# Moving the rotary and residual sums of a hybrid decoder block into transfers that add at their destination

## Chip, cores and metric

One core of a Trainium2 chip. The metric is the device time of one execution in microseconds (us); with one core its span is that time. The kernel is written for the engines PE (matmul), DVE (vector), ACT (scalar), POOL and SP (which only issues transfers).

## What is computed

One layer of a decoder block on 2048 tokens of width 1024, all in float32, and a final norm. Cut from the reference:

```
u = rms_norm(h, norm1_gain)
x_lru, g_lru, q, k, v, g_ret = split(u @ w_in)
y_lru = rms_norm(rg_lru(conv(x_lru)) * gelu(g_lru))
qh, kh = rotary(q), rotary(k)          # concat(x1*cos - x2*sin, x2*cos + x1*sin)
y_ret = head_group_norm(retention(qh, kh, v)) * silu(g_ret)
h = h + concat(y_lru, y_ret) @ w_out
a, v = split(conv(rms_norm(h) @ ffn_up_w))
h = h + (gelu(a) * v) @ ffn_down_w
return rms_norm(h, final_norm_gain)
```

The sums that the change is about are the one inside `rotary` and the two with `h + ...`.

## The kernel before

The tokens are two groups g = 0, 1 of 1024 columns; everything is kept transposed, as tiles of 128 features by 1024 tokens (512 KB). A float32 matmul is made of three products of high and low parts: ACT rounds a tile to its high part (`wh`, `bh`), DVE subtracts it to get the low one (`wl`, and `raw` or `bl` for the activations). This is `split`. The big products run in units of a 2 x 2 block scheme with seven products instead of eight (`Unit`, L589; `PlainUnit` with eight, L725). One product is 12 matmuls of 128 x 512. A `Unit` uses the PSUM banks x (one), y and e (two each), and its helper `out` empties them: `u2`, `c11`, `c22`, `c21`, `c12` each take one quadrant out of `py`, `px`, `py`/`pe`, `py` and `pe`.

The stages are A (input projection with the recurrence and the retention heads), B (output projection), U (up-projection), D (down-projection, in three chunks c of its inner dimension, each a pass over both groups). They run as A for both groups, B for both, U for both, then D for c = 0, 1, 2. In the traced run A ends near 582 us, B runs to about 770, U to about 1700, D to about 2150, and the rest is the end.

Two classes empty the banks. `PlainOut` (L853) copies them to an `o` tile on ACT and adds the `pe` part on DVE. `AddOut` (L920), used by B and D, first loads the tile to be added to into a slot `res` (from the input x in B, from DRAM tile `h` in D) and lets DVE add every quadrant from PSUM into it. In D with c = 0 or 1 the result is stored as the next version of `h` in DRAM; with c = 2 and in B it goes to the norm, whose `add` squares it on ACT (`sqt`, `sqacc`) and sums on DVE. In B the result is also stored as the first version of `h`.

`rotate` (L1211) in a retention head swaps the two halves of a q or k tile by two transfers on SP into `sw`, multiplies both by the sine and cosine rows and adds, three operations on DVE.

The order on every engine is not that of the source: a planner at build time (`Flow`, L198) takes tasks with due times, models each engine's clock with the costs `cost_pe`, `cost_v`, `cost_a`, `cost_p` (L131 to L163), a lag of 0.2 us between engines, a transfer rate `RATE` and `SLOTS` buffers, and writes the order down. A longer or shorter modelled cost therefore moves instructions on all engines. Operations all carry line L127 in the profile (the helper that records them), and transfers L365. On each engine instructions run in the order given, so one that waits holds up those behind it; each transfer queue has eight semaphores in turn.

Of the kernel before, what the change touches and what calls it, by code (L numbers as in the profile page):

```python
# [39 lines left out]
EPS = 1e-6  # L40
SLOTS = 55
BANKS = {"x": 1, "y": 2, "e": 2, "sm": 3}
# [63 lines left out]
class Engine:  # L106
# [24 lines left out]
    def cost_pe(self, op, n, args, kw):  # L131
        if op == "transpose":
            return 0.13
        one = max(0.03, 0.0133 + n / 2400)
        if args[1].shape[0] == 64:
            one /= 2
        return one if args[1].dtype == F32R else 4 * one

    def cost_v(self, op, n, args, kw):
        if op == "tensor_tensor_scan":  # L140
            return 0.2 + 2.1e-3 * n
        if op in ("tensor_scalar", "tensor_copy", "memset"):
            return 0.15 + 0.535e-3 * n
        if op == "reciprocal":
            return 0.15 + 6.1e-3 * n
        if op == "bn_stats":
            return 0.3
        if op == "scalar_tensor_tensor":
            return 0.2 + 1.06e-3 * n
        return 0.15 + 1.05e-3 * n  # L150

    def cost_a(self, op, n, args, kw):
        us = 0.17 + 0.86e-3 * n
        if isinstance(kw.get("scale"), bass.AP):
            us += 0.1
        if isinstance(kw.get("bias"), bass.AP):
            us += 0.09
        if "accum_out" in kw:
            us += 0.2
# [38 lines left out]
class Flow:  # L198
# [33 lines left out]
    def ready(self, op):  # L232
        t = 0.0
        for name in op.reads:
            w = self.wrote.get(name)
            if w:
                t = max(t, w[0] + (0.0 if w[1] == op.eng else 0.2))
        for name in op.writes:
            for table in (self.wrote, self.read):
                w = table.get(name)  # L240
                if w:
                    t = max(t, w[0] + (0.0 if w[1] == op.eng else 0.2))
        return t

    def issue(self, op, start):
        us = op.us
        if op.eng == "a" and op.func is not None and op.func not in ANY_TABLE and op.func not in self.table:
            self.table = next(t for t in TABLES if op.func in t)
            us += 1.28
# [4 lines left out]
        if op.eng == "pe":  # L254
            end += 0.1
# [72 lines left out]
def hymba_block_kernel(ctx: ExitStack, tc: tile.TileContext, xh, xn, win, wout, wup, down, gates, vecs,  # L328
# [30 lines left out]
    def dma(dst, src, queue="sp"):  # L359
        n = 1  # L360
        for d in dst.shape:
            n *= d
        start = (nc.scalar if queue == "a" else nc.sync).dma_start
        writes = [] if dst.tensor.name == yT.tensor.name else parts(dst)
        return Op(queue, lambda: start(dst, src), ISSUE, writes, parts(src), kb=n / 256)  # L365

    class Dram:
# [118 lines left out]
    z_d = [[Dram(f"z{g}_{i}") for i in range(2)] for g in range(NG)]  # L486
    h_d = [[[Dram(f"h{g}_{c}_{i}") for i in range(KT // 2)] for c in range(4)] for g in range(NG)]
    u_d = [Blocks(f"u{g}") for g in range(NG)]
# [430 lines left out]

    class AddOut:  # L920


        def __init__(self, src, done):
            self.src, self.done = src, done
            self.t = {}
            self.there = [Event(), Event()]

        def load(self, t0):
            def fn(i):
                yield Until(t0 - 8)  # L930
                self.t[i] = yield Slot("res")
                yield from self.src[i][0].get(self.t[i], self.src[i][1])
                self.there[i].on = True

            for i in range(2):
                fl.spawn(fn(i), t0 - 4 + i)

        def add(self, i, n, src):
            yield self.there[i]
            t = self.t[i][:, half(n)]  # L940
            yield v.tensor_tensor(out=t, in0=t, in1=src, op=ALU.add)

        def quadrant(self, m, n, ps):
            yield from self.add(m, n, ps)
            free(ps)
            self.quads[m, n] = True
            if (m, 0) in self.quads and (m, 1) in self.quads:
                yield from self.done(m, self.t[m])

        def piece(self, m, c0, c1, ps):  # L950
            yield self.there[m]
            t = self.t[m][:, c0:c1]
            yield v.tensor_tensor(out=t, in0=t, in1=ps[:, 0:c1 - c0], op=ALU.add)
            free(ps)
            yield from self.pieces(m, self.t[m], c0, c1)
# [10 lines left out]
        def c22(self):  # L966
            u = self.unit
            yield from self.add(1, 1, u.y)
            u.done["c22a"].on = True
            yield u.t0 + 5 - SOON  # L970
            yield from self.add(1, 1, u.e)
            u.done["c22b"].on = True

        def c21(self):
            yield from self.add(1, 0, self.unit.y)
            free(self.unit.y)
            yield self.unit.done["c22b"]
            yield from self.done(1, self.t[1])

        def c12(self):  # L980
            yield from self.add(0, 1, self.unit.e)
            free(self.unit.e)
            yield self.unit.done["c11"]
            yield from self.done(0, self.t[0])

# [215 lines left out]
    class Head:  # L1201
# [354 lines left out]
    def stage_b(g):  # L1556
        st = RawStage("B", g, m_d[g])
        ng = NormGroup(V_N2, u_d[g].put, h_d[g][0], LATE * g)
        us = []
        for m in (range(KT // 2) if g == 0 else reversed(range(KT // 2))):  # L1560
            ms = (m, m + KT // 2)
            src = [(x_d[g][k // 2], k % 2) for k in ms]
            us.append(PlainUnit(st, (wout[ms[0]], wout[ms[1]]), AddOut(src, lambda i, t, ms=ms: ng.add(ms[i], t))))
        return st, us
# [6 lines left out]
    def stage_d(g, c):  # L1571
# [8 lines left out]

        ng = FinalGroup(V_NF, None) if final else NormGroup(V_NF, store, h_d[g][3])

        def partial(m, t):
            yield from h_d[g][c + 1][m // 2].put(m % 2, t)
            free(t)

        us = []
        for m in (range(KT // 2) if g == c % 2 else (KT // 2 - 1, *range(KT // 2 - 1))):
            ms = (m, m + KT // 2)
            src = [(h_d[g][c][k // 2], k % 2) for k in ms]  # L1590
            done = (lambda i, t, ms=ms: ng.add(ms[i], t)) if c == 2 else (lambda i, t, ms=ms: partial(ms[i], t))
            out = AddOut(src, done)
            out.pieces = lambda i, t, c0, c1, ms=ms: ng.piece(ms[i], t, c0, c1)
# [59 lines left out]
def _layout(inputs):  # L1653
# [32 lines left out]
    cos, sin = np.cos(ang).T, np.sin(ang).T  # L1686
    rope = np.stack([np.concatenate([cos, cos]), np.concatenate([-sin, sin])]).astype(f32)
    rope = rope.reshape(2, P, S // HT, HT).transpose(2, 0, 1, 3)
# [31 lines left out]
```

## Time and profile before

| what | us |
|---|---|
| median of 3 runs (2165.2 to 2167.5) | 2167.2 |
| the profiled execution, its span | 2165.3 |
| PE busy | 2143.6 |
| DVE busy | 1729.8 |
| ACT busy | 1226.1 |
| POOL busy | 38.3 |

The granted clock of PE is 0.999 of full speed. The profiled execution is read as follows: rows of one instruction have the start, the duration, engine, line, operation and its destination and sources, and in brackets how long the engine stood idle before it and whom it waited for. Rows of a group have a count, then busy time, the mean ns of one, and the idle time before. A wait is named by what PE wrote and read, so `PE px <- DVE raw` is a matmul into `px` that waited for DVE's `raw`.

### The profile page before, as it was taken

To read this page: it belongs to the slowest core of one execution; us is meant where nothing else is said; L and a number is where in the kernel's file an instruction comes from. 1 tells how busy PE (TensorE), PEld (TensorE's weight loads), DVE (VectorE), ACT (ScalarE), POOL (GpSimd) and SP (SyncE) were. 2 spreads that over 40 slices of the span, in tenths; PEclk is the share of its full clock that TensorE was granted. 3 is DMA by queue.
4 is the path that set the end of the run, shared out by engine and by line. 5 is a ranking of instruction groups with operands and counts; after the bars stand their busy time and mean duration, and the time that the engine had idled before them with its cause. 6 is when DMAs were issued, how large, how long until landed. Compare 5 with 4: busy or idle time off the path is not lost.

```text
span 2165.3 us, 26460 instructions
## 1 busy us (share of the span) xinstructions
PE 2143.6 (99%) x9848; PEld 1768.5 (82%) x9848; DVE 1729.8 (80%) x2185; ACT 1226.1 (57%) x1768; POOL 38.3 (2%) x32
## 2 busy tenths in 40 slices
PE   9999999999999999999999999999999999999998
PEld 7878887888878888888888888888888888888887
DVE  6999896877854789988878988787878977777776
ACT  6774668555652266666666866666666544334432
POOL 0000000000000000000000000000000000000000
PEclk9999999999999999999999999999999999999999
DMA  8966444431657935544233432322335777667674
GB/s 327 377 210 226 141 163 118 160 111 58 226 185 275 390 132 180 185 141 156 98 106 128 175 127 98 122 98 100 105 107 185 260 299 261 232 255 278 237 258 189
DMA packets 140768, 404.69 MB, mean 187 GB/s; under 512 B 15920, under 2 KB 20448, under 8 KB 140640
## 3 DMA queue, kind: packets, MB, share of 16 engines
q1 hardware_dynamic: 139344, 401.96, 52.7%
q8 instruction: 77, 1.26, 0.2%
q10 hardware_dynamic: 1296, 1.05, 0.1%
q14 instruction: 51, 0.42, 0.1%
HBM read 269.49 MB, written 125.07 MB: 182 GB/s over the span
## 4 chain that ended last, share of the span: by engine, by line
PE 92%; DVE 3%; DMA 3%; issue 1%; ACT 0%; SPq 0%; POOL 0%; DVEq 0%; ACTq 0%
PE py L127 33%; PE px L127 22%; PE pe L127 21%; PE pq L127 12%; PE po L127 1%; DMA raw<-in_dram 1%; PE pa L127 1%; PE pk L127 1%; PE sc L127 1%; PE pt L127 1%; DVE o L127 0%; PE mst L127 0%; DMA xt<-in_dram 0%; DMA x<-in_dram 0%; DVE wl L127 0%
## 5 line engine op out<-in xcount | busy, mean ns | idle before, releaser
L127 DVE TENSOR_TENSOR wl<-s,wh 128x1024 fp32r<-128x1024 f32 x172 | 210.2, 1222 | 113.4 <-ACT wh L127 108.7
L127 PE MATMUL px<-bh,wh 128*128 128x512 f32 x728 | 285.4, 392 | 1.4 <-DVE res L127 1.4
L127 PE MATMUL py<-bh,wh 128*128 128x512 f32 x728 | 285.9, 393 | 0.0
L127 PE MATMUL px<-raw,wh 128*128 128x512 f32 x728 | 283.8, 390 | 1.8 <-DVE raw L127 1.8
L127 PE MATMUL py<-bh,wl 128*128 128x512 f32 x728 | 283.9, 390 | 1.3 <-DVE wl L127 1.3
L127 PE MATMUL pe<-bh,wh 128*128 128x512 f32 x728 | 285.1, 392 | 0.0
L127 PE MATMUL pe<-raw,wh 128*128 128x512 f32 x728 | 283.7, 390 | 0.9 <-DVE raw L127 0.9
L127 PE MATMUL pe<-bh,wl 128*128 128x512 f32 x728 | 283.8, 390 | 0.7 <-DVE wl L127 0.7
L127 PE MATMUL py<-raw,wh 128*128 128x512 f32 x728 | 283.7, 390 | 0.0
L127 PE MATMUL px<-bh,wl 128*128 128x512 f32 x728 | 283.6, 390 | 0.0
L127 DVE SCALAR_TENSOR_TENSOR c<-o,vec,c 128x1022 f32<-128x1022 f32 x192 | 244.0, 1280 | 8.1 <-ACT c L127 3.3
L127 ACT CAST wh<-s 128x1024 fp32r<-128x1024 f32 x172 | 180.4, 1049 | 122.1 <-DVE s L127 107.1
L127 PE MATMUL py<-bh,wv 128*128 128x512 f32 x728 | 240.5, 391 | 1.9 <-DVE res L127 1.0
L127 ACT COPY o<-py 128x512 f32<-128x512 f32 x204 | 119.7, 587 | 167.1 <-PE py L127 163.5
L127 ACT CAST bh<-raw 128x1024 fp32r<-128x1024 f32 x158 | 162.2, 1050 | 68.0 <-DMA h<-res 27.4
L127 DVE TENSOR_TENSOR raw<-raw,bh 128x1024 fp32r<-128x1024 f32 x158 | 188.7, 1219 | 9.2 <-ACT bh L127 9.1
L127 PE MATMUL pq<-bh,wh 128*128 128x512 f32 (+1 forms) x432 | 168.0, 389 | 0.5 <-ACT bh L127 0.4
L127 PE MATMUL pq<-bh,wl 128*128 128x512 f32 (+1 forms) x432 | 165.2, 382 | 0.5 <-DVE wl L127 0.5
L127 PEld LDWEIGHTS py<-bh,wh 128*128 128x128 f32 x728 | 136.7, 188 | 33.1 <-issue 3.0
L127 PEld LDWEIGHTS py<-bh,wv 128*128 128x128 f32 x728 | 136.7, 188 | 32.7 <-ACT o L127 1.5
L127 PEld LDWEIGHTS px<-bh,wh 128*128 128x128 f32 x728 | 136.7, 188 | 31.3 <-DVE res L127 1.8
L127 PEld LDWEIGHTS py<-bh,wl 128*128 128x128 f32 x728 | 136.7, 188 | 30.8 <-DVE wl L127 2.1
(143 smaller groups left out, 3775.0 us busy)
## 6 DMA issues: line engine op xcount, KB each, us to landing
wa<-in_dram SPq DMA_DIRECT2D x86, 512.0 KB, 4.4
wb<-in_dram SPq DMA_DIRECT2D x86, 512.0 KB, 5.3
h<-res SPq DMA_DIRECT2D x56, 512.0 KB, 3.7
g_T<-t SPq DMA_DIRECT2D x96, 256.0 KB, 2.5
raw<-g_T SPq DMA_DIRECT2D x48, 512.0 KB, 5.7
res<-h SPq DMA_DIRECT2D x48, 512.0 KB, 7.2
g<-c SPq DMA_DIRECT2D x76, 256.0 KB, 4.2
raw<-g SPq DMA_DIRECT2D x38, 512.0 KB, 6.7
```

Of the source, the lines that this page charges most:

```text
L127: return Op(self.name, lambda: fn(*args, **kw), us, writes, reads, func=func)
```

## The change

Rotary: DVE multiplies the tile by the sine row into `sw` and by the cosine row in place, and two transfers issued by Pool add the halves of `sw`, swapped, into the tile (the sign of the sine row is set for that). Residual sums: `AddOut` becomes a `PlainOut`, so ACT copies the quadrants and DVE adds the `pe` part; a finished tile is then added by one transfer from Pool. In B and in D with c = 2 the transfer adds x or `h` from DRAM into the tile; in D with c = 0, 1 it adds the tile to `h` in DRAM, which is then one version only. The pieces of the `LastUnit` keep the old way. The planner's costs and lags are set to other numbers and there are 54 slots. The core of the diff:

```diff
-SLOTS = 55
+SLOTS = 54
...
+LAG = {"pe": 0.21, "v": 0.13, "a": 0.15, "p": 0.13, "dma": 0.08}
...
-        return 0.15 + 1.05e-3 * n
+        us = 0.068 + n / (1920 if op in ("tensor_scalar", "tensor_copy", "memset") else 960)
+        if any(isinstance(kw.get(k), bass.AP) for k in ("scalar", "scalar1")):
+            us += 0.06
+        return us
...
-        us = 0.17 + 0.86e-3 * n
...
+        us = 0.11 + (0.735e-3 if args[1].space == bass.MemoryType.PSUM else 0.82e-3) * n + 0.095 * aps
...
     def cost_p(self, op, n, args, kw):
-        return 0.1 if op == "dma_start" else max(1.0, 0.3 + 2.2e-3 * n)
+        return 0.8 + 0.105 * n if n < 16 else 0.15 + 2.25e-3 * n
...
-                t = max(t, w[0] + (0.0 if w[1] == op.eng else 0.2))
+                t = max(t, w[0] + (0.0 if w[1] == op.eng else LAG[w[1]]))
...
+    def add_to(dst, src):
...
+        return Op("p", lambda: nc.gpsimd.dma_start(dst, src, accum_op=ALU.add), 1.2, parts(dst), parts(dst) + parts(src),
+                  kb=n / 256)
...
-    class AddOut:
+    class AddOut(PlainOut):
...
-        def quadrant(self, m, n, ps):
-            yield from self.add(m, n, ps)
...
-        def u2(self):
-            yield from self.add(0, 1, self.unit.y)
-            self.unit.done["u2"].on = True
-
-        def c11(self):
-            yield from self.add(0, 0, self.unit.x)
-            free(self.unit.x)
-            self.unit.done["c11"].on = True
...
+        def first(self):
+            return self.whole(0, self.t1)
+
+        def second(self):
+            return self.whole(1, self.t2)
+
+        def whole(self, i, t):
+            d, j = self.src[i]
+            yield d.there[j]
+            if self.done is None:
+                yield add_to(d.t[:, j], t)
+                free(t)
+            else:
+                yield add_to(t, d.t[:, j])
+                yield from self.done(self.ms[i], t)
...
         def rotate(self, name, x):
-            sw = yield Slot("sw")
-            yield dma(sw[0:64], x[64:128]) + dma(sw[64:128], x[0:64])
...
+            sw = yield Slot("sw")
+            yield v.tensor_tensor(out=sw, in0=x, in1=sn, op=ALU.mult)
             yield v.tensor_tensor(out=x, in0=x, in1=cs, op=ALU.mult)
-            yield v.tensor_tensor(out=sw, in0=sw, in1=sn, op=ALU.mult)
-            yield v.tensor_tensor(out=x, in0=x, in1=sw, op=ALU.add)
+            yield add_to(x[0:64], sw[64:128]) + add_to(x[64:128], sw[0:64])
             free(sw)
...
-    nc = _bacc.Bacc("TRN2", target_bir_lowering=False, num_devices=1, dynamic_dma_scratch_size=256)
+    nc = _bacc.Bacc("TRN2", target_bir_lowering=False, num_devices=1, dynamic_dma_scratch_size=2048)
```

In the order of the engines PE keeps its matmuls. DVE gives up the 16 sums of the rotary and the 92 additions from `py` and `px` in D and those from `pq` in B; SP gives up the swaps and the loads of `res`. The 94 adding transfers (32 of half a tile, 62 of a tile) stand on Pool. On PE two places at the ends move: the broadcast `pb` at the start stands behind 120 matmuls, and at the end the first pair of `mst` stands behind the last twelve 256-wide matmuls instead of ahead of them.

The first place is SP at the end of stage B for group 1. A `w` is a weight tile of the last unit, `h1` are the stores of group 1's finished rows, `u0` the stores of group 0's normed rows, `in_0` the input x, `in_3` the weights. Before:

```order
L365 DMA u0_T4_1_136<-t34_6075 128x512
L365 DMA u0_22_1_138<-h_5910 128x512
L365 DMA h1_0_1_110<-res_5762 128x1024
L365 DMA res_5927<-in_0_dram 128x1024
L365 DMA h1_0_3_112<-res_5764 128x1024
L365 DMA w_6007<-in_3_dram 128x1024
L365 DMA res_6094<-in_0_dram 128x1024
L365 DMA w_6095<-in_3_dram 128x1024
```

The same place on SP in the changed kernel:

```order
L361 DMA u0_T4_1_120<-t34_6035 128x512
L361 DMA u0_22_1_122<-h_5887 128x512
L361 DMA h1_1_98<-o0_5920 128x1024
L361 DMA h1_3_100<-o1_6009 128x1024
L361 DMA w_5963<-in_3_dram 128x1024
L361 DMA w_6054<-in_3_dram 128x1024
L361 DMA raw_5964<-u0_11_0_109 128x1024
```

Both stores of `h1` now precede both loads of `w`, with no load of `res` between them, and the stores' tiles `o0_5920` and `o1_6009` are the ones that the adding transfers on Pool complete.

The second place is ACT in the last chunk of D, where a unit ends and the next one begins (the `sqt` and `sqacc` are the squares for the final norms, the copy `py<-px` is the start of a unit's y bank). Before:

```order
L127 ACTIVATE sqt_16021<-res_15673 128x1024
L127 CAST wh_16041<-wa_16035 128x1024
L127 COPY py_16071<-px_16056 128x512
L127 CAST wh_16091<-s1_16054 128x1024
L127 ACTIVATE sqt_16127<-res_15833 128x1024
L127 CAST wh_16142<-s1_16054 128x1024
L127 CAST wv_16147<-wb_16037 128x512
L127 ACTIVATE sqt_16150<-res_15832 128x1024
```

The same stretch of ACT in the changed kernel:

```order
L128 ACTIVATE sqacc_15932<-o1_15845 128x1024
L128 COPY o0_15946<-py_15863 128x512
L128 ACTIVATE sqt_15984<-o0_15810 128x1024
L128 COPY o0_15946<-px_15847 128x512
L128 CAST wh_15968<-wa_15963 128x1024
L128 COPY o1_15983<-py_15863 128x512
L128 COPY py_16003<-px_15988 128x512
L128 CAST wh_16009<-s1_15969 128x1024
L128 COPY o1_15983<-py_15863 128x512
```

The square of `o0_15810`, which the adding transfer completes, now stands between the copies of the next unit's quadrants `o0_15946` from `py` and from `px`; the latter frees the only x bank. Two more such places follow, for `o0_15946` and `o0_16216`.

More of the change, by code (lines that the diff above doesn't have):

```diff
@@ L132, in cost_pe @@
         if op == "transpose":
[L133 to L137, printed above, removed]
+            return 0.11
+        if args[1].dtype == F32R:
+            return 0.0133 + n / 2400
+        one = max(0.111, 0.0266 + n / 1200)
+        return one * (1.23 if args[1].shape[0] == 64 else 2)
     def cost_v(self, op, n, args, kw):
         if op == "tensor_tensor_scan":
-            return 0.2 + 2.1e-3 * n
-        if op in ("tensor_scalar", "tensor_copy", "memset"):
-            return 0.15 + 0.535e-3 * n
+            return 0.3 + 2.04e-3 * n
         if op == "reciprocal":
             return 0.15 + 6.1e-3 * n
[L146 to L149, printed above, removed]
-        return 0.15 + 1.05e-3 * n
+        us = 0.068 + n / (1920 if op in ("tensor_scalar", "tensor_copy", "memset") else 960)
+        if any(isinstance(kw.get(k), bass.AP) for k in ("scalar", "scalar1")):
+            us += 0.06
+        return us
     def cost_a(self, op, n, args, kw):
-        us = 0.17 + 0.86e-3 * n
-        if isinstance(kw.get("scale"), bass.AP):
+        aps = sum(isinstance(kw.get(k), bass.AP) for k in ("scale", "bias"))
+        us = 0.11 + (0.735e-3 if args[1].space == bass.MemoryType.PSUM else 0.82e-3) * n + 0.095 * aps
+        func = next((x for x in args if isinstance(x, AF)), None)
+        if aps and func is not None and func not in ANY_TABLE:
             us += 0.1
-        if isinstance(kw.get("bias"), bass.AP):
-            us += 0.09
         if "accum_out" in kw:
-            us += 0.2
+            us += 0.1
         return us
     def cost_p(self, op, n, args, kw):
-        return 0.1 if op == "dma_start" else max(1.0, 0.3 + 2.2e-3 * n)
+        return 0.8 + 0.105 * n if n < 16 else 0.15 + 2.25e-3 * n
 class Event:
@@ L241, in ready @@
                 if w:
-                    t = max(t, w[0] + (0.0 if w[1] == op.eng else 0.2))
+                    t = max(t, w[0] + (0.0 if w[1] == op.eng else LAG[w[1]]))
         return t
@@ L486, in hymba_block_kernel @@
     z_d = [[Dram(f"z{g}_{i}") for i in range(2)] for g in range(NG)]
-    h_d = [[[Dram(f"h{g}_{c}_{i}") for i in range(KT // 2)] for c in range(4)] for g in range(NG)]
+    h_d = [[Dram(f"h{g}_{i}") for i in range(KT // 2)] for g in range(NG)]
+    e_d = [[Dram(f"e{g}_{i}") for i in range(KT // 2)] for g in range(NG)]
     u_d = [Blocks(f"u{g}") for g in range(NG)]
@@ L930, in fn @@
                 yield Until(t0 - 8)
-                self.t[i] = yield Slot("res")
-                yield from self.src[i][0].get(self.t[i], self.src[i][1])
+                self.res[i] = yield Slot("res")
+                yield from self.src[i][0].get(self.res[i], self.src[i][1])
                 self.there[i].on = True
[L935 to L941, printed above, removed]
@@ L943, in quadrant @@
-        def quadrant(self, m, n, ps):
-            yield from self.add(m, n, ps)
[L945 to L948, printed above, removed]
+            if type(self.unit) is LastUnit:
+                for i in range(2):
+                    fl.spawn(fn(i), t0 - 4 + i)
         def piece(self, m, c0, c1, ps):
             yield self.there[m]
-            t = self.t[m][:, c0:c1]
+            t = self.res[m][:, c0:c1]
@@ L974, in c21 @@
[L974 to L984, printed above, removed]
+            yield from self.pieces(m, self.res[m], c0, c1)
+        def first(self):
+            return self.whole(0, self.t1)
@@ L1562, in stage_b @@
             src = [(x_d[g][k // 2], k % 2) for k in ms]
[L1563 removed]
+            us.append(PlainUnit(st, (wout[ms[0]], wout[ms[1]]), AddOut(g, ms, src, ng.add)))
         return st, us
@@ L1579, in store @@
                 free(pair[j])
[L1581 to L1585, printed above, removed]
+        ng = FinalGroup(V_NF, None) if final else NormGroup(V_NF, store, e_d[g])
         us = []
@@ L1589, in stage_d @@
             ms = (m, m + KT // 2)
-            src = [(h_d[g][c][k // 2], k % 2) for k in ms]
-            done = (lambda i, t, ms=ms: ng.add(ms[i], t)) if c == 2 else (lambda i, t, ms=ms: partial(ms[i], t))
-            out = AddOut(src, done)
+            src = [(h_d[g][k // 2], k % 2) for k in ms]
+            out = AddOut(g, ms, src, ng.add if c == 2 else None)
             out.pieces = lambda i, t, c0, c1, ms=ms: ng.piece(ms[i], t, c0, c1)
```

25 lines of the change are left out of this document (9 added, 16 removed).

## The prediction

> **What bounds the kernel now.** I read the first two rows of the page, then the waits of PE, then the busy time in 25-us stretches, and last single rows at the places the change touches. First the page: engines with busy time and share.
>
> ```profile
> span 2165.3 us, 26460 instructions
> PE 2143.6 (99%) x9848; PEld 1768.5 (82%) x9848; DVE 1729.8 (80%) x2185; ACT 1226.1 (57%) x1768; POOL 38.3 (2%) x32
> ```
>
> PE is busy in 2143.6 of 2165.3 us, and the change leaves its matmuls the same, so at most 21.7 us can be had. Of those the waits of PE hold a part (what it wrote and read, whom it waited for; us in total, times, longest); shown are the eleven largest of fourteen.
>
> ```profile
> PE px L127 <- DVE raw L127: 1.8, 1, 1.8
> PE y L127 <- DVE z L127: 1.5, 1, 1.5
> PE pb L127 <- POOL ms L127: 1.4, 2, 1.1
> PE px L127 <- DVE res L127: 1.4, 1, 1.4
> PE py L127 <- DVE wl L127: 1.3, 2, 1.0
> PE mst L127 <- DVE sqacc L127: 1.2, 1, 1.2
> PE py L127 <- DVE res L127: 1.0, 1, 1.0
> PE pt L127 <- DVE o L127: 0.9, 1, 0.9
> PE pe L127 <- DVE raw L127: 0.9, 1, 0.9
> PE py L127 <- ACT o L127: 0.8, 2, 0.4
> PE pe L127 <- DVE wl L127: 0.7, 1, 0.7
> ```
>
> These are 12.9 us, and 8.0 of them name DVE inside the stages (all but `z` at the start, `pb` and `mst` of the norms, and ACT's `o`). Where DVE is late is seen in the stretches (length, then busy PE, PEld, DVE, ACT, POOL with counts, PE clock, DMA share, GB/s).
>
> ```profile
> 150.00:175.00 25.00, 23.24 (x101) 18.38 (x100) 22.23 (x26) 8.72 (x13) 0.00 (x0) 1.00 0.97 301
> 725.00:750.00 25.00, 25.00 (x112) 20.72 (x111) 10.78 (x13) 6.34 (x7) 0.00 (x0) 1.00 1.01 385
> 1700.00:1725.00 25.00, 24.14 (x107) 19.58 (x105) 24.68 (x30) 8.19 (x10) 0.00 (x0) 1.00 0.50 170
> 2100.00:2125.00 25.00, 23.98 (x106) 19.57 (x105) 22.97 (x25) 7.16 (x8) 0.00 (x0) 1.00 0.93 344
> 1700.00:2150.00 450.00, 446.75 (x2017) 370.96 (x2016) 336.17 (x400) 170.94 (x189) 2.75 (x2) 1.00 0.68 248
> ```
>
> The clock is 1.00 throughout. In the down-projection (1700 to 2150) PE loses 3.25 us, with DVE packed where it loses them and ACT busy 171 of 450 us. In the out-projection around 725 PE loses nothing, but the DMA engines are full (share 1.01).
>
> **The change part by part.** The profiled execution spans 2165.3 us and the median of the runs is 2167.2, so I take the sum as a difference and apply it to the median. What a measurement of this kernel can tell from no change is about 0.2%, 4.3 us.
>
> *Residual sums of the down-projection.* DVE loses these additions from PSUM, and ACT gains copies of the kind in the third row.
>
> ```profile
> L127 DVE TENSOR_TENSOR res<-res,py 128x512 f32<-128x512 f32 x69 | 47.3, 685 | 32.0 <-PE py L127 31.6
> L127 DVE TENSOR_TENSOR res<-res,px 128x512 f32<-128x512 f32 x23 | 15.8, 685 | 18.9 <-PE px L127 18.9
> L127 ACT COPY o<-py 128x512 f32<-128x512 f32 x204 | 119.7, 587 | 167.1 <-PE py L127 163.5
> 1739.68 0.50 PE L127 MATMUL px<-bh,wh 128*128 128x512 f32 x1 [1.37 <-DVE res L127]
> 2123.79 0.47 PE L127 MATMUL py<-bh,wv 128*128 128x512 f32 x1 [1.02 <-DVE res L127]
> 1709.59 0.51 PE L127 MATMUL pe<-raw,wh 128*128 128x512 f32 x1 [0.86 <-DVE raw L127]
> ```
>
> DVE gives up 92 x 0.685 = 63.0 us of its 336; ACT takes 92 x 0.587 = 54.0 us and stands then at 225 of 450. The two waits on `res` were for PSUM banks that DVE had not yet emptied; ACT is idle more than half the time, so they go (1.4 + 1.0). The wait on `raw` came where DVE was busy 24.68 of 25 us, and it goes too (0.9). Together -3.3 us; the bounds are -3.3 and 0, the latter if other work is late there next. The additions with `pe` stay on DVE.
>
> *What the last third of that stage pays.* There the square of a finished row-block on ACT needs the sum that the adding transfer makes, and in the order of ACT three of the squares stand between the next unit's copy from `py` and its copy from `px` (shown with the change). While ACT waits for the transfer, the one x bank is not freed. The same moments in the trace of before, for one unit: the last addition into a finished tile, the addition from `px`, and the next product into the x bank.
>
> ```profile
> 2036.65 0.68 DVE L127 TENSOR_TENSOR res<-res,pe 128x512 f32<-128x512 f32 x1
> 2041.94 0.69 DVE L127 TENSOR_TENSOR res<-res,px 128x512 f32<-128x512 f32 x1 [0.90 <-PE px L127]
> 2044.46 0.39 PE L127 MATMUL px<-bh,wh 128*128 128x512 f32 x1
> L127 ACT ACTIVATE sqt<-res 128x1024 f32<-128x1024 f32 x26 | 27.6, 1061 | 80.4 <-DVE res L127 69.1 <-PE px L127 4.4 <-DVE s L127 4.0
> ```
>
> The tile is complete at 2036.65 + 0.68 = 2037.33; the bank must be free at 2044.46. Square and copy take 1.06 + 0.59, so the adding transfer may take 7.13 - 1.65 = 5.5 us, and every us beyond it is one us of PE, at three places. No adding transfer is in this trace. The nearest rows are plain transfers of the same size or half of it (median us from issue to landing), and Pool's short instruction:
>
> ```profile
> h<-res SPq DMA_DIRECT2D x56, 512.0 KB, 3.7
> res<-h SPq DMA_DIRECT2D x48, 512.0 KB, 7.2
> sw<-o SPq DMA_DIRECT2D x32, 256.0 KB, 3.8
> L127 POOL TENSOR_TENSOR rs<-rs,cst 128x4 f32<-128x4 f32 x16 | 20.6, 1285 | 426.1 <-DVE rs L127 426.1
> ```
>
> An adding transfer both reads and writes; a short Pool instruction takes 1.3 us, which I take as the bound for what an issue costs Pool. The ends are 3.7, no cost, and 7.2 + 1.3 = 8.5, 3 x 3.0 = 9 us. A transfer whose sum lands in SBUF reads DRAM like `res<-h`, but `res<-h` was issued early and often queued with others, so I take a landing just past the limit at one place: +0.5 us. (A gain is excluded here: the bank was free in time before.)
>
> *Rotary.* Before, two transfers swap halves, then DVE multiplies twice and adds; now DVE multiplies twice and two transfers from Pool add.
>
> ```profile
> L127 DVE TENSOR_TENSOR o<-o,sw 128x1024 f32<-128x1024 f32 x16 | 19.6, 1224 | 0.4
> 387.53 0.63 PE L127 MATMUL pt<-idt,o 128*128 128x128 f32 x4 [0.93 <-DVE o L127]
> 550.23 7.68 DMA sw<-o
> ```
>
> DVE loses 16 x 1.224 = 19.6 us in the first 582 us. I let go the 1.8 us wait on `raw`, where DVE was the engine waited for and nothing else was named, and half of the 2.0 us of waits on `wl`, since the stretch 150 to 175 has both DVE (22.23 of 25) and the DMA engines (0.97) nearly full: -2.8 us, between 0 and -3.8. The price is latency. Before: a swap of 3.8 and two DVE steps in line after it, 3.8 + 2.4 = 6.2 us. Now: two DVE steps, 2.4, and a transfer of 3.8 plus the 1.3 of a second issue, 7.5 us, so 1.3 later. One head's transposes waited already (0.93), and the chain that ended last holds a swap of 7.68 us, so the old way was not always in time either; the 1.3 is paid there at least; one such head is +1.2 us. If all eight heads waited as long, it would be 10 us; if the queue on SP that is no longer in the way saves as much, it is -0.9.
>
> *Residual sums of the out-projection.* x is added from DRAM into the tile by Pool, and the store of the sum to `h` on SP waits for it. In group 1 that store now stands right ahead of the last two loads of weights (shown with the change). The row of before with the load's issue, and the subtraction that needs it:
>
> ```profile
> 732.13 0.40 SPq L365 DMA_DIRECT2D w<-in_dram  x1
> 742.94 1.22 DVE L127 TENSOR_TENSOR wl<-w,wh 128x1024 fp32r<-128x1024 f32 x1
> 747.77 0.69 DVE L127 TENSOR_TENSOR res<-res,pq 128x512 f32<-128x512 f32 x1 [2.48 <-PE pq L127]
> ```
>
> The unit that uses them starts when the one before has ended, about 747.8; the low part is there at 744.2, so 3.6 us of cover. A SP that waits for a landing of 3.7 to 8.5 us takes some of it; the ends are 0 and 4.9 (8.5 - 3.6). Since the loads of `res` no longer stand between the weights, I take +0.5. If that cover is gone, each us costs one.
>
> [...] The nearest row to an adding transfer is the store of the same bytes, 3.7 us; at that length the two places above cost 0 and 3.7 - 3.6 = 0.1 us, and my 1.0 for both is room for one queue. [...]
>
> *Start, end, and the up-projection.* The broadcast `pb` of the first norm is placed later at the start: -0.4 at most of the 1.4 in two pieces. At the end the second `mst` pair stands behind the last 12 narrow matmuls instead of the first pair ahead of them, so nothing is left to fill the wait of the norm; the wait was this:
>
> ```profile
> 2155.67 0.58 PE L127 MATMUL mst<-ones,sqacc 128*128 128x1 f32 x4 [1.15 <-DVE sqacc L127]
> ```
>
> I take +0.5, between 0 and 1.2. The up-projection has no row of waits and none of the new work; nothing.
>
> Sum: -3.3 - 2.8 + 1.2 + 0.5 + 0.5 - 0.4 + 0.5 = -3.8 us; 2167.2 - 3.8 = 2163.4.
>
> **The rivals.** *Late sums (slower).* Each adding transfer takes twice what the store takes, 7.4 us. For it: `res<-h`, 7.2, the same bytes in the other direction, is as long; the DMA engines are at 0.93 to 1.01 in two of the stretches where the sums are wanted. Against: between 1700 and 2150 the mean share is 0.68, and each sum replaces a load of the same size. It decides from a landing of 5.5 us in the down-projection, 3.6 in the out-projection. Price: three holds of ACT, 3 x (7.4 - 5.5) = 5.7, and the last weights, 7.4 - 3.6 = 3.8, in place of my 0.5 + 0.5: -3.8 - 1.0 + 9.5 = +4.7, so 2171.9. [...]
>
> *Hidden anyway.* The new order of every engine puts other work late in place of what went: DVE keeps 273 of 450 us, and the conversions of the activations and weights are still in the same line. For it: in 1700 to 1725 DVE was full without regard to one operation. Against: PE waits only at three places there. Half of the gains stay, the prices as above: -3.0 + 2.3 = about -0.7, so 2166.5.
>
> *All waits go.* With measured durations the order fits the machine, and of the 12.9 us all but the start and end pieces (1.5, 1.4, 1.2) go, 8.8 us, with nothing new: 2158.4. For it: the waits are few and short. Against: three kinds of new dependence on transfers.
>
> That the sums are not made by transfers at all is excluded: Pool issues 94 in the new order, and the additions are missing from DVE's.
>
> **How the numbers follow.** Likeliest 0.45, with a range of its own of 2160.5 to 2166.5; late sums 0.23; hidden anyway 0.18; all waits go 0.14. The range goes from 2157, just under the last, to 2173, which holds the late sums at their price but not at both ends (9 and 4.9). Faster by over 4.3 us is all of the last case and somewhat over half of the likeliest's chance below 2162.9: 0.14 + 0.24 = 0.38 and 0.02 of the hidden case, 0.40. Slower by over 4.3 is most of the late sums, 0.19. The rest, 0.41, is the same.
>
> **What would show it.** Right: in the waits of PE no `res` and no `raw` after 1700; adding transfers landing under 5.5 us; the rows of DVE lighter by 63 and 19.6 us; U unchanged. Wrong: waits of PE for ACT's `o` or `px` between 2000 and 2130 (late sums), a wait for `wl` or `wh` near 748, or waits of `pt` in the first 580 us of several us; or the waits on `raw` and `wl` as large as now (hidden).

## The result

The changed kernel takes 2252.0 us (2248.9 to 2256.3, 4 runs) where the kernel before takes 2167.0: 1.040 times as long, with a 95% interval of 1.038 to 1.041. The forecast was 2163.4.

First the head of the profile page of the changed kernel.

```profile
span 2251.1 us, 26585 instructions
PE 2172.5 (97%) x9848; PEld 1785.9 (79%) x9848; DVE 1640.0 (73%) x2045; ACT 1280.7 (57%) x1891; POOL 125.3 (6%) x126
```

The span is 85.8 us longer. PE does the same matmuls but is busy 28.9 us longer, and it is idle 78.6 us where it was idle 21.7, 56.9 more. DVE is relieved by 89.8 us, and the rows that the forecast named (63.0 and 19.6 us) are gone; the kernel is slower all the same.

Where the time went is read from the timeline of PE, at the first matmul of each stage (A input projection and heads, B output projection, U up-projection, D down-projection up to the last narrow unit). All lengths are us. The border of U and D is the same matmul in all kernels, 0.9 us ahead of D's first. The times are medians of the runs; e5, e13 and e14 were run once. The lengths are those of one profiled execution, which in e4 and e6 took 6 us less than the median. In A e9, e13 and e14 have the same order on every engine and yet took 612.2, 608.7 and 607.3 us, so a difference of 5 us in A between two kernels that wait there tells nothing.

| kernel | time | A | B | U | D |
|---|---|---|---|---|---|
| before | 2167.0 | 582.1 | 187.3 | 915.0 | 445.0 |
| changed | 2252.0 | 619.2 | 209.0 | 915.0 | 471.7 |
| e1 rotary as before | 2241.7 | 608.3 | 207.6 | 915.0 | 474.1 |
| e2 residual sums as before | 2202.1 | 616.9 | 189.4 | 915.0 | 442.8 |
| e3 numbers and 54 buffers only | 2184.6 | 599.4 | 187.1 | 915.0 | 442.7 |
| e4 changed, landing planned as 8 us | 2213.6 | 606.4 | 187.8 | 921.5 | 453.8 |
| e5 changed, plain copies for sums | 2210.8 | 609.3 | 195.4 | 915.0 | 453.1 |
| e6 all sums, old numbers | 2248.0 | 608.3 | 203.7 | 915.3 | 476.8 |
| e7 e6, landing planned as 8 us | 2213.2 | 606.7 | 188.2 | 922.0 | 453.3 |
| e8 lags and 54 buffers only | 2189.9 | 602.6 | 187.1 | 915.0 | 446.4 |
| e9 54 buffers only | 2195.8 | 612.2 | 187.3 | 915.0 | 444.3 |
| e10 costs and 54 buffers only | 2187.8 | 600.5 | 191.2 | 915.0 | 442.8 |
| e11 numbers, 55 buffers | 2189.8 | 603.1 | 187.1 | 915.0 | 445.4 |
| e12 new numbers from late U on | 2166.5 | 581.1 | 187.3 | 915.0 | 443.7 |
| e13 e9 and sums into DRAM in D | 2202.8 | 608.7 | 187.3 | 915.0 | 454.1 |
| e14 e13, landing planned as 8 us | 2195.4 | 607.3 | 187.3 | 915.0 | 448.1 |
| e15 before, rate 331 | 2166.7 | 582.7 | 187.3 | 915.3 | 444.6 |
| e16 before, lag 0.19 | 2170.5 | 586.5 | 187.3 | 915.0 | 443.5 |

The changed kernel loses 37.1 us in A, 21.7 in B, nothing in U, 26.7 in D. The waits of PE in A (20 to 619 us), the largest two:

```profile
PE pt L128 <- DMA o<-sw: 20.9, 6, 5.8
PE py L128 <- ACT o L128: 11.1, 5, 3.7
```

In B (619 to 829):

```profile
PE pq L128 <- ACT wh L128: 7.6, 1, 7.6
PE mst L128 <- DVE sqacc L128: 3.9, 2, 2.0
```

And in D (1743 to 2215):

```profile
PE py L128 <- ACT o L128: 11.6, 7, 2.9
PE px L128 <- ACT o L128: 6.0, 2, 3.6
```

None of these stood in the list of before but for `py <- ACT o`, 0.8 us, and `mst <- DVE sqacc`, 1.2 us at the end. The waits on `res` and on `raw` in D are gone, as forecast. The DMA view gives how long the adding transfers took, median us from issue to landing:

```profile
h<-o POOLq DMA_DIRECT2D x32, 512.0 KB, 7.5
o<-sw POOLq DMA_DIRECT2D x32, 256.0 KB, 8.0
o<-in_dram POOLq DMA_DIRECT2D x16, 512.0 KB, 7.2
o<-h POOLq DMA_DIRECT2D x14, 512.0 KB, 6.8
```

All lie past the 5.5 us from which the forecast said that ACT's squares would hold up PE; it worked that limit out for one place in D. One of the forecast places, in the last chunk of D, from the timelines of Pool (the issue), ACT and PE:

```profile
2083.68 0.87 POOL L368 DMA_DIRECT2D o<-h  x1 [4.53 <-DVE o L128]
2091.57 1.06 ACT L128 ACTIVATE sqt<-o 128x1024 f32<-128x1024 f32 x1 [5.63 <-DMA o<-h]
2092.54 0.57 ACT L128 COPY o<-px 128x512 f32<-128x512 f32 x1
2093.16 0.79 PE L128 MATMUL px<-bh,wh 128*128 128x512 f32 x1 [2.40 <-ACT o L128]
```

The square starts 7.89 us after the issue, the copy that frees the x bank comes only behind it, and PE waits 2.40 us for the bank: 7.89 - 5.5 is 2.4. The other forecast place is the last weights of B, with their issue on SP:

```profile
789.78 1.37 SPq L361 DMA_DIRECT2D h<-o  x2
792.11 2.33 SPq L361 DMA_DIRECT2D w<-in_dram  x2
```

They are issued from 792.1 on, and PE stops at 795.6 for 7.6 us; before, they were issued 15 us ahead of their unit. It was not the two stores of `h1` in front of them that held SP up by waiting for their sums: Pool issued those at 764.4 and 774.8, they had landed by 784.1, and the stores came at 789.8. What SP waited for from 770 to 800 was led by earlier stores of its own queue, and no `o<-in_dram` is in the list:

```profile
SPq L361 <- DMA u_T<-t: 6.9, 13, 1.7
SPq L361 <- DMA u<-h: 4.7, 10, 1.9
```

SP came late because the norm of group 0 did, whose 28 stores of normed rows stand ahead of these weights. That norm did wait for a sum: its issue on Pool, the square on ACT, the matmul of the norm on PE, and the row of statistics on SP.

```profile
724.85 0.86 POOL L368 DMA_DIRECT2D o<-in_dram  x1 [7.03 <-ACT o L128]
730.65 1.06 ACT L128 ACTIVATE sqt<-o 128x1024 f32<-128x1024 f32 x1 [2.39 <-DMA o<-in_dram]
733.11 2.53 PE L128 MATMUL mst<-ones,sqacc 128*128 128x1 f32 x16 [1.96 <-DVE sqacc L128]
741.76 0.28 SPq L995 DMA_DIRECT2D row<-rb  x1
```

That row went out 122.6 us into B, and 108.8 in the kernel before (at 690.90); the weights went out 172.9 us into B, and 150.0 before.

What the waits do not show is the clock. Around one wait of 5.8 us (180 to 194 us; the seventh number is the granted clock):

```profile
180.00:182.00 2.00, 2.00 (x10) 1.59 (x9) 1.09 (x1) 0.88 (x1) 0.00 (x0) 1.00 1.08 231
184.00:186.00 2.00, 0.00 (x0) 0.00 (x0) 0.17 (x1) 1.82 (x3) 0.00 (x0) 0.67 1.06 240
188.00:190.00 2.00, 1.56 (x6) 1.49 (x7) 1.54 (x2) 0.43 (x1) 0.00 (x0) 0.50 0.69 272
190.00:192.00 2.00, 2.00 (x7) 1.53 (x7) 0.00 (x0) 1.77 (x3) 0.00 (x0) 0.62 0.00 0
192.00:194.00 2.00, 2.00 (x12) 1.67 (x11) 0.88 (x2) 0.68 (x2) 0.00 (x0) 1.00 0.00 0
```

The clock drops to half while PE waits and stays there for 3.1 us of work after it. The record of the granted clock has thirteen stretches at half clock, with 51.7 us of PE's work in them; the kernel before has one, at its end, with none. Within them a 128x512 matmul starts 0.43 us after the one ahead of it and at full clock 0.23 us (medians of the changed kernel), so about half of that work's time, by this estimate 25.9 us, is lost, which is most of the 28.9 us that PE is busy longer for the same matmuls and nearly a third of the whole loss.

### The profile page after: what moved, and what is told of

It is laid out like the page before. It is cut to its first block, busy times and chain, and to the rows that moved or that the text cites. A ratio compares the mean times of both kernels' runs of the same rounds, so it can differ in the third digit from the quotient of the medians.

```text
span 2251.1 us, 26585 instructions
## 1 busy us (share of the span) xinstructions
PE 2172.5 (97%) x9848; PEld 1785.9 (79%) x9848; DVE 1640.0 (73%) x2045; ACT 1280.7 (57%) x1891; POOL 125.3 (6%) x126
## 3 DMA queue, kind: packets, MB, share of 16 engines
q8 instruction: 77, 1.26, 0.2%
## 4 chain that ended last, share of the span: by engine, by line
PE 71%; DMA 11%; DVE 7%; issue 6%; ACT 4%; POOL 1%; SPq 0%; DVEq 0%; POOLq 0%; ACTq 0%
PE py L128 26%; PE pe L128 18%; PE px L128 17%; PE pq L128 7%; DMA o<-sw 3%; DMA h<-o 1%; DMA w<-in_dram 1%; DVE xc L128 1%; DVE o L128 1%; DMA o<-h 1%; DMA wa<-in_dram 1%; DVE wl L128 1%; PE pt L128 1%; ACT wh L128 1%; ACT o L128 1%
## 5 line engine op out<-in xcount | busy, mean ns | idle before, releaser
L128 ACT COPY o<-py 128x512 f32<-128x512 f32 x273 | 158.7, 581 | 213.6 <-PE py L128 188.7
L128 DVE TENSOR_TENSOR wl<-wa,wh 128x1024 fp32r<-128x1024 f32 x86 | 105.2, 1223 | 113.1 <-ACT wh L128 111.8
L128 ACT ACTIVATE c<-o,vec 128x1024 f32<-128x1024 f32 x96 | 119.6, 1245 | 88.1 <-DVE o L128 87.0
```

Source lines behind the costliest of these rows:

```text
L128: return Op(self.name, lambda: fn(*args, **kw), us, writes, reads, func=func)
```

## The experiments

The theory after this reading: the sums land after 7 to 8 us, the planner had counted on 1.7 us and the bytes at its rate (2.5 to 3.3 us), and engines that run in order stand behind whoever waits. Its rivals: the planner's new numbers make a worse order by themselves, or the transfers load the DMA engines so much that everything is late.

**e1, the rotary alone as before.**

```diff
-            yield v.tensor_tensor(out=sw, in0=x, in1=sn, op=ALU.mult)
+            yield dma(sw[0:64], x[64:128]) + dma(sw[64:128], x[0:64])
...
-            yield add_to(x[0:64], sw[64:128]) + add_to(x[64:128], sw[0:64])
+            yield v.tensor_tensor(out=x, in0=x, in1=sw, op=ALU.add)
```

> The changed kernel with the rotary alone as before (swap on SP, three operations on DVE); the residual sums, costs and buffers stay changed. Late-sums theory (adding transfers land after 7 to 8 us, the planner counted on 2.5 to 3.3, and engines that run in order stand behind the ones that wait): stage A, 37 us longer in the changed kernel than before, comes back, the rest stays: 2252 - 35 = about 2217 us, with no wait of PE for o<-sw. Costs theory (the new numbers of the planner make a worse order by themselves): within 10 us of 2252.

Measured 2241.7 us, 10 and not 35 less. The waits on `o<-sw` are gone, but A keeps 26 of its 37 us, on other waits. Most of A's loss is there without the rotary's sums.

**e2, the residual sums alone as before** (`AddOut`, `h_d`, `stage_b` and `stage_d` of the kernel before).

> The changed kernel with the residual sums alone as before (loads of res, additions on DVE from PSUM); the rotary still by adding transfers. Late-sums theory: B (22 us longer in the changed kernel) and D (27 us) come back, A stays 37 us long: about 2252 - 48 = 2204 us. Costs theory: within 10 us of 2252. Together with the rotary run the two parts should add up to the 85 us, to about 10.

Measured 2202.1 us, as the theory had it: B and D come back to 189.4 and 442.8, A does not (616.9). The losses of B and D belong to the residual sums. With the rotary's 10.4 us the two parts make 60 and not 85 us, so something else costs too.

**e3, the new numbers alone**, with 54 buffers in the kernel before.

```diff
-SLOTS = 55
+SLOTS = 54
...
+LAG = {"pe": 0.21, "v": 0.13, "a": 0.15, "p": 0.13, "dma": 0.08}
```

> The kernel before with the new costs, lags and 54 buffers alone, no adding transfer. Late-sums theory: within 5 us of before, 2162 to 2172. Costs theory: more than 40 of the 85 us, 2205 or more.

Measured 2184.6 us (1.008, 1.007 to 1.010): both theories miss. There is no adding transfer in this kernel, and A is 17.3 us longer; D is 2.3 shorter.

**e4, a true duration.** One number of the planner is added to the changed kernel.

```diff
+        op.land = 8.0
...
+            end = max(end, start + op.land)
```

> The changed kernel, with one number of the planner changed: an adding transfer is taken to land 8.0 us after its issue, as measured, and not after 2.5 to 3.3. The same 94 adding transfers. Late-sums theory (the planner's wrong duration put their readers too early): most of the 85 us go, under 2190 us, the waits of PE for o<-sw and of ACT's copies under a third. Contention theory (the transfers cost the DMA engines so much that everything is late, wherever it stands): over 2220 us.

Measured 2213.6 us (1.021, 1.019 to 1.023): 38 of the 85 us go, which is between the two expectations, and PE still waits 11.8 us for `o<-sw` and 13.8 for ACT's copies, about half and not under a third. B is 187.8, all of its loss gone, with the transfers landing just as late (7.9 us for `o<-in_dram`) in the stage where the DMA engines are fullest (mean share 0.78). So in B the load of the DMA engines is not what decided; the order was. A keeps 24 us and D 9. In U 6.5 us come up at its start, where PE waited for `raw` on DVE, with the clock at 0.63 to 0.94 behind it.

**e5, copies in place of sums**, the changed kernel in the same order, with the sums left out of the result.

```diff
-        return Op("p", lambda: nc.gpsimd.dma_start(dst, src, accum_op=ALU.add), 1.2, parts(dst), parts(dst) + parts(src),
+        return Op("p", lambda: nc.gpsimd.dma_start(dst, src), 1.2, parts(dst), parts(dst) + parts(src),
```

> The changed kernel with its 94 transfers from Pool as plain copies: the same order, sizes and waits, but nothing is added at the destination (the sums are left out). If adding is what makes them slow: landing falls from 7 to 8 us to about 4, the waits on o<-sw nearly go, and the time falls by 30 us or more, to under 2222. If it is the issue from Pool or the load of the DMA engines: landing within 1 us of 7 to 8, time within 15 us of 2252.

Measured 2210.8 us in one run, 41 less. Landing, in the DMA view of this kernel:

```profile
h<-o POOLq DMA_DIRECT2D x32, 512.0 KB, 5.0
o<-sw POOLq DMA_DIRECT2D x32, 256.0 KB, 7.3
o<-in_dram POOLq DMA_DIRECT2D x16, 512.0 KB, 5.4
o<-h POOLq DMA_DIRECT2D x14, 512.0 KB, 5.4
```

The time is that of the first expectation, the landing lies between the two: whole tiles land 1.4 to 2.5 us sooner, the halves of the rotary hardly. Medians mix two things, adding and load, and they come apart when the transfers are sorted by how busy the DMA engines were in the 3 us behind each issue (medians in us of the 3 to 21 transfers with a landing on record):

| transfer | share under 0.6 | share over 0.9 |
|---|---|---|
| store of a tile from SP, kernel before | 2.6 | 4.7 |
| copy of a tile to DRAM from Pool, e5 | 2.9 | 5.6 |
| sum of a tile to DRAM from Pool, changed | 5.7 | 7.6 |
| copies of a tile into SBUF from Pool, e5 | 3.9 | 6.9 to 7.4 |
| sums of a tile into SBUF from Pool, changed | 5.4 to 5.7 | 8.8 to 9.6 |
| rotary's half, copy in e5 | 3.1 | 8.1 |
| rotary's half, sum in the changed kernel | 3.5 | 8.4 |

By these medians adding costs a whole tile 1.5 to 2.8 us, and 5.4 to 5.7 is what a sum takes even where little else moves: about the limit of 5.5. A copy from Pool costs 0.3 to 0.9 us more than SP's store. The halves are late with the load and not by the adding: 21 of 32 are issued where the DMA engines are full. D falls from 471.7 to 453.1 and B from 209.0 to 195.4, which fits copies of 5.0 to 5.4 that lie under the limit of the one place; for the other places that limit was not worked out.

**e6 and e7, all sums with the old costs and lags**, without and with the landing of 8 us.

> The changed kernel with the costs and lags of before (and 54 buffers): all adding transfers, the planner's old numbers. If costs (17 us by themselves, all of it in stage A) and transfers add: 2252 - 17 = 2235 us. If the old, longer numbers had given the transfers' readers room: under 2215.

> The same with the adding transfer taken to land after 8.0 us: the adding transfers with old costs and their own measured duration. If the parts add: 2213.6 - 17.5 = 2196 us. If a true duration was all that was missing once the costs are the old ones: within 10 us of before, 2157 to 2177, and then the adding itself costs nothing.

Measured 2248.0 (2242.2 and 2253.9) and 2213.2 us (1.022, 1.020 to 1.024); neither expectation of either run came true. The costs of the change do not add up as in the first reading: with the old numbers the sums cost the same. B is again mended by the true duration, A is 608 and 607 in both. A true duration is not all that was missing.

**e8, e9, e10, e11, the rest of A.** New lags alone, 54 buffers alone, new costs alone (each with 54 buffers), and all new numbers with 55. None has an adding transfer.

> The kernel before with the new lags between engines (and without the extra 0.1 us of a matmul) and 54 buffers, old costs. If the loss of the new numbers is the missing margin between engines: most of the 17.5 us, 2178 to 2186. If it is in the costs of the operations: 2162 to 2172.

> The kernel before with 54 buffers in place of 55, nothing else. Costs and lags theory (the 17 to 23 us that the new numbers cost in stage A come from the numbers): 2164 to 2171. Buffer theory (the tables were run with 54 buffers too, and stage A is short of buffers): 2178 or more, most of the 17 us.

> The kernel before with the new costs of the operations and 54 buffers, old lags; with the run of the lags alone (+23 us) it splits the numbers. Missing margin in the lags: within 6 us of before. Shuffle theory: 10 to 25 us slower as well, so that the two do not add up to the 17 us of both.

> The kernel before with the new costs and lags and its 55 buffers. Costs and lags theory: still 10 us or more slower, 2177 to 2187. Buffer theory: back within 5 us of before. Shuffle theory (any change of the numbers draws a new order of stage A, and before's was a lucky or tuned one): slower by some other amount, with the waits at other places than with 54 buffers.

Measured 2189.9, 2195.8 (1.013, 1.011 to 1.014), 2187.8 and 2189.8 us (1.010, 1.009 to 1.012). One buffer less, nothing else, costs 29 us, all of it in A; the new numbers with all 55 buffers cost 23. All with 54 buffers lose 17 to 30 us in A, in no order of addition. With the new numbers the missing buffer costs nothing (54 in e3 are 5.2 us faster than 55 in e11), so 29 us is what one order lost by it and not the worth of a buffer. Where it loses them is seen on ACT in the run with 54 buffers alone:

```profile
174.92 0.58 ACT L127 COPY o<-py 128x512 f32<-128x512 f32 x1 [12.05 <-DMA x<-x]
```

The two largest waits of PE in the same run:

```profile
PE py L127 <- ACT o L127: 14.4, 5, 6.2
PE pe L127 <- DVE o L127: 8.2, 1, 8.2
```

The copy that empties a bank waits 12 us until a store has let go of the buffer that it writes, and PE waits 6.2 of them. The same diff that gives the buffer up sets `dynamic_dma_scratch_size` from 256 to 2048; that the one needs the other is not shown, and the changed kernel with 55 buffers was not run.

**e12, the new numbers only where they helped** (from 1600 us of the plan on, 55 buffers, no adding transfer).

> The kernel before with 55 buffers and old numbers up to 1600 us of the plan, and the new costs and lags from there: stage A as before, stage D as in the run with the new numbers alone (442.7 in place of 445.0 us). If the gain in D is real: 2163 to 2165.5, the only version faster than before. If D's gain hangs on what went before it: 2166 to 2168.

Measured 2166.5 us against 2166.9 for the kernel before beside it, ratio 1.000 (0.999 to 1.001). D is 1.3 us shorter in the trace, which the time cannot tell from nothing. No version that was run beats the kernel before.

**e13 and e14, sums into DRAM that nobody reads soon.** The run with 54 buffers alone (e9), plus the 32 sums of the first two chunks of D; the order up to D is that of e9.

```diff
+            yield add_to(d.t[:, j], t)
+            free(t)
+            d.summed[j].on = self.last
```

> The kernel before with 54 buffers and old numbers, and only the 32 sums of the first two chunks of stage D made by transfers that add to h in DRAM; the rotary, B and the last chunk as before. Its order is that of the run with 54 buffers alone up to stage D, so stage D compares directly (444.6 us there). If only readers that wait for a sum cost time (nobody reads these for a long while): D at 441 to 446. If a buffer held until the sum has landed costs as well (planner: 3.3 us, landing 7.5): D at 450 or more, with ACT's conversions waiting for h<-o.

> The same with the landing taken as 8.0 us by the planner. If the held buffers were the cost and a true duration mends it: D at 441 to 446 us. If the DMA engines are what is short in D: 450 or more.

D was 454.1 and 448.1 us, against 444.3 (444.6 in the expectation, which took D's border 0.3 us earlier). So sums without an early reader cost 9.8 us in D too, and with a true duration 3.8, which is between the two expectations and too little to be told from nothing in single executions; the whole kernels took 7.0 us more than e9 and 0.4 less. The waits of ACT in D of the run without the true duration name why (what ACT wrote, whom it waited for):

```profile
ACT bh L127 <- DMA h<-o: 21.9, 6, 6.5
ACT o L127 <- DMA h<-o: 7.2, 1, 7.2
```

A transfer that reads `o` is named as what `bh` waits for: the next user of the buffer is planned into it 4 us too early (3.3 us, landing 7.7), and ACT, in order, holds the bank-emptying copies behind it. PE's wait for such copies, which e9 does not have in D, and one of the four places where it follows:

```profile
PE py L127 <- ACT o L127: 8.7, 6, 3.0
1857.48 2.94 ACT L127 CAST bh<-raw 128x1024 fp32r<-128x1024 f32 x3 [5.46 <-DMA h<-o]
1860.33 0.58 ACT L127 COPY o<-py 128x512 f32<-128x512 f32 x1
1860.95 0.79 PE L127 MATMUL py<-bh,wh 128*128 128x512 f32 x1 [2.97 <-ACT o L127]
```

**e15 and e16, changes that mean nothing**: the planner's rate 331 for 330, or its lag 0.19 for 0.20, in the kernel before.

> The kernel before, with the planner's transfer rate 331 in place of 330: a change that means nothing, with 55 buffers and no adding transfer. Shuffle theory (the order of stage A before is an exceptionally good draw): 10 to 25 us slower, A at 592 to 607 us in place of 582. Buffer and numbers theory (54 buffers and the new costs are each worse in themselves): within 5 us of before, A at 580 to 587.

> The kernel before, with the planner's lag between engines 0.19 in place of 0.20 us: a second draw that means nothing. Shuffle theory: 10 to 25 us slower, at other places than with the rate of 331. Buffer and numbers theory: within 5 us of before.

Measured 2166.7 (1.000, 0.999 to 1.001) and 2170.5 us (1.002, 1.001 to 1.003). So A's order before is not spoiled by any small change: these two cost 0 and 3.5 us. They are small, though. Up to the end of A, e15 has another instruction than before at 15 of 505 places on ACT and 10 of 737 on DVE, e16 at 117 and 149; one buffer less (e9) at 291 and 334, all new numbers (e11) at 322 and 509. That any order so far from before's loses 17 to 30 us, whatever moved it, is not excluded.

## Why the prediction was wrong

Wrong in sign and in size. The step that failed with most us behind it is the price of a sum that lands late. The forecast put +0.5 us on the squares in D, +0.5 on the last weights of B and +1.2 on the rotary; without the residual sums the kernel is 49.9 us faster (e2), without the rotary's 10.4 (e1). The step that had no term at all is 54 buffers with the new numbers, 17.5 us by themselves (e3). By its steps:

- *The DVE relief in D* held as far as it can be seen: no `res` and no `raw` in the waits after 1700. Whether it was worth 3.3 us is not shown, since other waits came in their place.
- *The squares in D* failed in size. The mechanism, the place and the limit of 5.5 us were right; the landing was taken as just past the limit at one place (+0.5 us), and it is 6.8 in the median. The forecast also stopped at the readers of a sum. In the chunks without a reader the buffer that the transfer reads is itself held until it has landed, and e13 has D 9.8 us longer with that alone. D lost 26.7.
- *The rotary* failed in size: a landing of 3.8 + 1.3 was taken from a swap issued on SP, and the pairs from Pool land after 8.0: most are issued where the DMA engines are full, and there they take 8.4 (3.5 where they are not). PE waited 20.9 us for them in six places, not 1.2. How much of A's 37 us that is stays open: with the new numbers, the rotary's sums added 17.5 us to A (e2 against e3), with the old ones and all sums, -3.9 (e6 against e9), which is within what A differs by for one order.
- *The last weights of B* were the right place with too small a price (7.6 us of wait, +0.5 forecast), and in part the wrong reason. The forecast had SP wait for the sums of the two stores; those had landed. The sums held up the squares on ACT and so the norms: there are 4.7 us of waits for `sqacc` and `ms`, which the forecast did not have, and half clock behind them, and the norm's stores then made SP late. These waits are nearly gone in e4 (B 187.8), so they too came from the late sums. The cover of 3.6 us was computed from the old issue at 732, and the new order issues the weights 3 us before they are needed.
- *What was given no term*: 54 buffers and the new numbers. They stood in the diff, and the forecast treated them as free, and even as a gain ("all waits go", 0.14). By themselves, without any adding transfer, they cost 17.5 us together, and 21 to 29 in the four other runs of parts of them.
- *The clock*, named as 1.00 throughout, was taken to stay so. It fell at 12 of the 15 waits of 1.9 us or more in the changed kernel, and 25.9 us, by the estimate above, went to work at half clock.
- *Start, end and up-projection* held: the end is 0.2 us longer (+0.5), U is unchanged.
- *The rivals.* Late sums came true, at 0.23, in D for the reason given, but its price of +4.7 counted four places; each place cost more and there were many. That a sum takes about twice the store's 3.7 us is what the medians show (6.8 to 7.5); at like load it is the adding (5.7 against 2.9) and hardly Pool (2.9 against 2.6). Against plain copies in the same order (e5) the landing of whole tiles grows by 1.26 to 1.5 times in the medians (5.4 to 6.8, 5.4 to 7.2 and 5.0 to 7.5 us).
- *Two slips in the working* change little: one late head is 1.3 us and stands in the sum as 1.2, and 2162.9 lies below the likeliest value, so less than half of that case's chance lies under it, not "somewhat over half".

What stays open is how A's loss divides among buffers, numbers and rotary sums, since they do not add, and why the planner's measured durations order A worse than its old, longer ones.

## What to carry to other kernels

A transfer that an engine waits for has to be planned at its measured landing, and the buffer that it reads stays taken until then as well: with both at 8 us for about 3, B lost 0.5 us in place of 21.7 although the same transfers ran. What a change takes silently (here one of 55 buffers, and the planner's numbers) can cost more than the change was forecast to bring, so it gets a term of its own. And where PE waits about 2 us or more, the wait has to be counted with the work at half clock that can follow it: the 51.7 us of such work in the changed kernel lost about half their time.

## What was not expected of the hardware

The forecast had the clock stay at 1.00. Half clock came after a wait as short as 1.83 us, and like waits fall on either side. One and the same wait of PE for `raw` in stage A is 1.82 us in the kernel before and 1.83 with 54 buffers; granted clock in the seventh number. Before:

```profile
118.36:121.77 3.41, 2.49 (x11) 1.72 (x10) 3.31 (x15) 2.85 (x5) 1.01 (x1) 1.00 0.43 145
121.77:125.18 3.41, 2.51 (x13) 1.66 (x13) 3.41 (x5) 1.50 (x4) 0.00 (x0) 1.00 0.82 283
```

With 54 buffers:

```profile
120.54:123.95 3.41, 1.58 (x7) 1.03 (x6) 3.38 (x6) 2.12 (x6) 0.71 (x1) 1.00 0.72 217
123.95:127.36 3.41, 3.41 (x11) 1.72 (x10) 3.41 (x6) 1.80 (x3) 0.00 (x0) 0.50 0.60 240
127.36:130.77 3.41, 3.41 (x16) 2.52 (x15) 3.41 (x4) 3.35 (x5) 0.00 (x0) 1.00 0.00 0
```

These windows are not chosen freely. The 81 stretches at half clock in the 18 traces, the last one of each trace at its end left out, are 3.41, 6.83 or 10.24 us long, and within a trace they start on one grid: in the changed kernel 22, 35, 68, 125 and so on up to 586 steps of 3.413 us behind the first. With 54 buffers the wait lies within one window of the grid, PE is idle in 1.83 of its 3.41 us, and the next window runs at half clock. In the kernel before an edge cuts the wait in two (its grid is counted back from its one stretch at half clock, at 2159.53), PE is idle in about 0.9 us of each window, and the clock stays. Over all traces, of the windows that began at full clock with PE idle for 1.95 us or more, 62 of 62 were followed by half clock (in the changed kernel alone 11 of 11); from 1.75 to 1.95 us 12 of 23 (2 of 3), from 1.0 to 1.75 us 3 of 94 (1 of 16). So the wait of 2.92 us at 2047 of the changed kernel left the clock alone because an edge cut it into 1.64 and 1.28. By an estimate from these counts a wait of 3.9 us or more (twice 1.95) is paid for wherever it lies, and for one between about 1.8 and 3.9 it depends on where the edge falls. In the changed kernel half clock followed all four waits over 3.9 us (4.32 to 7.59) and eight of the eleven from 1.91 to 3.73.
